# Batch-norm matmul on one core: the second block of w loaded ahead of the second half of the first chunk

## The chip, the cores and the metric

The kernel runs on one core of a Trainium2 chip. The metric is device time in microseconds of one execution, and the median over several executions is compared. The engines of the core are named as the profile names them: PE is TensorE (its matmuls; PEld are its weight loads), DVE is VectorE, ACT is ScalarE, POOL is GpSimd and SP is SyncE. POOL and SP issue the DMAs.

## What is computed

x holds 16 x 512 rows of 1024 numbers, weight is 1024 x 768, all float32. The product of all 8192 rows with the weight is normalised per output column over all rows:

```python
y = np.matmul(x, weight)
mean = np.mean(y, axis=(0, 1), keepdims=True)
var = np.var(y, axis=(0, 1), keepdims=True)
y_norm = (y - mean) / np.sqrt(var + eps)
return (gamma * y_norm + beta).astype(np.float32)
```

The statistics need every row, so nothing can be stored before the whole product is there. The kernel keeps the product on chip in bfloat16 and normalises it from there.

## The kernel before, in words

The 8192 rows are cut into 16 chunks of 512 rows (`CH`, `C`). The 768 output columns are six tiles of 128 (`NT`). The contraction over 1024 is cut into four blocks, counted by `jw`; a block has two halves (`e`), so that a full product of one output tile with one chunk is eight matmuls accumulating in one PSUM bank.

**Loads.** `load_x` (line 157) loads a range of rows with four DMAs from POOL, each of a quarter of the columns into 32 partitions, and the DMA converts to bfloat16. The first two chunks come in four loads of 256 rows each (called quarters of x below; the first two quarters are the two halves of chunk 0), the others in loads of 512 rows. `load_w` (line 145) loads one or more blocks of the weight, again with four DMAs from POOL. In all, w is loaded in three steps: block 0, block 1, and blocks 2 and 3 together. All these DMAs go out on one queue in program order; the framework gives them eight semaphores in turn, so a DMA is issued only when the one eight places before it has landed. That makes POOL wait, and what stands behind it on POOL waits too.

**Turning x.** x arrives with its rows on the partitions, while the matmuls need the contraction there; `turn_x` (line 164) transposes it on DVE, in squares of 32 x 32 pairs of bfloat16 numbers, into `xT`. For each half of chunk 0 there are two transposes: the first covers blocks 0 and 1, the second blocks 2 and 3.

**Matmuls.** `mm` (line 192) multiplies one output tile by one chunk, over a list of blocks and, for chunk 0, over a half of its rows: with `q0` and `q1` it covers 256 or all 512 columns of the moving operand. `mm_rows` (line 182) is the other form, with x as the stationary operand and 384 output columns at once; most chunks use it for the first three tiles. `wake` (line 151) runs matmuls on an idle tile that nobody reads, 30 at the very start and 8 (`FILL`) within chunk 0.

**The order.** Nothing is issued where it is written. Each piece of work is put into a list with a time that a small model in the code works out (`at`, line 441), the list is sorted by that time, and the pieces are then issued in that order; `seq` (line 77) ties each instruction behind the one before it on its engine. The model's times (2.7 us per 256 rows of x, 2.1 us per block of w and so on) decide only the order, never an actual wait. Lines 447 to 471 fix the order of the loads, and lines 497 to 510 that of chunk 0: `part(w, q0, q1, jws)` puts out the six tiles' matmuls for the halves q0 to q1 with the blocks `jws`, no earlier than the model has that block and those rows. Before the change the sequence on PE is: 30 idle matmuls, block 0 on the first half (12 matmuls of 256 columns), 8 idle matmuls, block 0 on the second half (12 of 256), block 1 on both halves at once (12 of 512), blocks 2 and 3 on both halves (24 of 512), then chunk 1.

**What follows.** Six tiles of chunk 0 fill six PSUM banks. As each is complete, DVE takes its statistics (`bn`) and ACT copies it out (`keep`). The remaining chunks follow on PE without a pause, the later tiles of chunks 5 to 15 last, while the finished tiles are normalised and stored.

Of the kernel before, what the change touches and what calls it, by code (L numbers as in the profile page):

```python
# [10 lines left out]
def kernel(  # L11
# [429 lines left out]
    def at(t, fn, *args):  # L441
        events.append((t, len(events), fn, args))
# [1 line left out]
    Q_US, MM_US, ROW_US = 2.7, 1.75, 1.31  # L444
    t = 1.0
    arrive = {}
    order = [("x", 0), ("w", 0, 1), ("x", 1), ("w", 1, 2), ("w", 2, 4)]
    order += [("x", q) for q in range(2, SHORT * QPC)] + [("c", c) for c in range(SHORT, C)]
    for kind, n, *n1 in order:
        if kind == "w":  # L450
# [46 lines left out]
    def part(w, q0, q1, jws):  # L497
        nonlocal pe
        pe = max(pe, arrive["w", w], arrive[q1 * QR // P - 1])
        for nt in range(NT):  # L500
            at(pe, mm, nt, 0, jws, q0, q1)
            pe += MM_US * len(jws) / JW * (q1 - q0) / QPC

    part(0, 0, 1, [0])
    at(pe, wake, FILL)
    part(0, 1, 2, [0])
    part(1, 0, 2, [1])
    pe = max(pe, arrive["w", 2])
    for nt in range(NT):
        unit(nt, 0, MM_US / 2, [2, 3])  # L510
# [148 lines left out]
```

## Time and profile before

| | |
|---|---|
| median of 6 runs | 217.39 us (217.07 to 217.72) |
| the profiled execution's own time | 217.72 us |
| its span, first to last instruction | 215.9 us |
| PE busy | 198.4 us, 92% of the span |
| DVE, ACT, POOL busy | 150.1, 124.0, 140.4 us |
| share of PE in the chain that ended last | 84% |
| start of the matmuls with blocks 2 and 3 | 20.07 us into the span |
| mean granted TensorE clock | 0.977 |

The profile shows one execution, times in microseconds from the first instruction. A row of the timeline merges instructions of one kind that follow one another: start, length, engine, line, operation with its tiles, the count, and in brackets how long the engine had been idle and what ended that. The chain of waits follows the last instruction back to what released it, step by step; it is read here in order of time. DMA rows name the tile written and the tensor read, with "landing" counted from the issue.

### The profile page before, as it was taken

What the parts mean: (1) busy time and instruction counts of PE and PEld (TensorE: products, weight loads), DVE (VectorE), ACT (ScalarE), POOL (GpSimd) and SP (SyncE); (2) the same over time, 40 slices, a digit from 0 to 9 for tenths busy, and PEclk for the clock granted to TensorE, in tenths of its full rate; (3) what the DMA queues carried; (4) which work ended last, traced back from release to release, by engine and by line L of the source; (5) the groups of instructions that cost most, each with busy time, mean ns of one, the idle gap of its engine ahead of it and who ended that gap; (6) DMA issues with size and microseconds to landing.
All of it is one profiled execution on the core that took longest, in us unless ns stands there. A gap on an engine that the chain in (4) does not pass through costs nothing.

```text
span 215.9 us, 3477 instructions
## 1 busy us (share of the span) xinstructions
PE 198.4 (92%) x1174; PEld 106.2 (49%) x1174; DVE 150.1 (70%) x261; ACT 124.0 (57%) x236; POOL 140.4 (65%) x158
## 2 busy tenths in 40 slices
PE   7797999999999999999999999999999999996900
PEld 2352454545455565566556554444445455554800
DVE  3220968886987999799854349988999896566800
ACT  2000563645464566357766513767759999987940
POOL 7786868678595999667558601999999996000000
PEclk9999999999999999999999999999999999999785
DMA  5999999999999999997000000689698999999997
GB/s 58 169 178 176 190 196 196 196 197 196 196 191 193 197 196 196 196 197 107 2 3 0 0 0 0 231 310 340 248 334 279 366 357 335 324 346 307 346 345 216
DMA packets 70178, 43.75 MB, mean 203 GB/s; under 512 B 4112, under 2 KB 69648, under 8 KB 70160
## 3 DMA queue, kind: packets, MB, share of 16 engines
q0 software_dynamic: 34624, 18.36, 62.3%
q1 hardware_dynamic: 35536, 25.18, 36.0%
q8 instruction: 9, 0.15, 0.3%
q14 instruction: 9, 0.07, 0.1%
HBM read 36.71 MB, written 25.17 MB: 287 GB/s over the span
## 4 chain that ended last, share of the span: by engine, by line
PE 84%; DMA 5%; POOL 3%; ACT 2%; issue 1%; DVE 0%; ACTq 0%; POOLq 0%
PE y_ps L196 44%; PE y_ps L186 31%; PE o_ps L414 7%; DMA w_sb<-in_weight_dram 3%; DMA ring<-in_x_dram 2%; POOL w_sb L149 2%; POOL ring L162 1%; ACT o_sb L427 1%; PE y_ps L332 1%; PE a_ps L274 1%; PE tot_ps L232 1%; ACT ring L427 0%; ACTq L654 0%; ACT y_sb L342 0%; DVE y_sb L400 0%
## 5 line engine op out<-in xcount | busy, mean ns | idle before, releaser
L196 PE MATMUL y_ps<-xT_sb,w_sb 128*128 128x512 bf16 (+1 forms) x460 | 111.4, 381 | 2.9 <-DMA w_sb<-in_weight_dram 2.6
L196 PEld LDWEIGHTS <-w_sb 128*128 128x128 bf16 x460 | 43.5, 96 | 59.0 <-issue 4.9
L186 PE MATMUL y_ps<-w_sb,xT_sb 128*128 128x384 bf16 x416 | 68.6, 326 | 0.0
L345 ACT CAST y_sb<-y_ps 128x512 bf16<-128x512 f32 x56 | 33.0, 589 | 47.0 <-DVE stats L318 44.8
L186 PEld LDWEIGHTS <-xT_sb 128*128 128x128 bf16 x416 | 40.7, 98 | 27.7
L162 POOL DMA_DIRECT2D ring<-in_x_dram x72 | 45.2, 634 | 12.6 <-DVE xT_sb L174 6.3
L318 DVE BATCH_NORM_STATS2 stats<-y_ps 128x6 f32<-128x512 f32 x55 | 37.2, 686 | 21.4 <-PE y_ps L196 21.4
L212 POOL TENSOR_TENSOR sum<-sum,sq_sb 128x384 f32<-128x384 f32 x41 | 41.1, 1002 | 15.2 <-ACT sq_sb L208 13.4
L174 DVE STREAM_TRANSPOSE xT_sb<-ring 128x1024 f32<-128x1024 f32 (+1 forms) x34 | 39.6, 1170 | 15.6 <-DMA ring<-in_x_dram 15.1
L291 POOL TENSOR_TENSOR ring<-ring,sum 128x768 f32<-128x768 f32 x19 | 34.6, 1847 | 12.0 <-DVE y_sb L390 12.0
L414 PE MATMUL o_ps<-ident,y_sb 128*128 128x128 bf16 x228 | 37.7, 230 | 2.1 <-DVE y_sb L400 2.1
L215 DVE TENSOR_TENSOR sum<-y_ps,sum 128x384 f32<-128x384 f32 x52 | 28.3, 544 | 12.6 <-ACT sq_sb L208 11.5
L208 ACT ACTIVATE sq_sb<-y_ps 128x384 f32<-128x384 f32 x52 | 25.5, 494 | 13.1 <-PE y_ps L186 10.0
L221 ACT CAST y_sb<-y_ps 128x384 bf16<-128x384 f32 x52 | 24.9, 478 | 12.3 <-DVE sum L215 12.3
L427 ACT CAST ring<-o_ps 128x1024 f32<-128x1024 bf16 (+1 forms) x22 | 21.1, 966 | 4.9 <-PE o_ps L414 3.6
L414 PEld LDWEIGHTS <-y_sb 128*128 128x128 bf16 x228 | 20.0, 103 | 4.1 <-DVE y_sb L400 2.2
L285 DVE TENSOR_TENSOR ring<-y_sb,a_ps 128x768 f32<-128x768 bf16 x19 | 17.7, 937 | 0.0
L379 ACT ACTIVATE y_sb<-y_sb,shift,scale 128x512 bf16<-128x512 bf16 x22 | 17.2, 815 | 0.0
L291 POOL TENSOR_TENSOR o_sb<-o_sb,sum 128x768 f32<-128x768 f32 x7 | 12.9, 1844 | 0.2 <-DVE o_sb L285 0.2
L155 PE MATMUL idle_ps<-idle_sb 128*128 128x512 bf16 x38 | 10.1, 430 | 1.2 <-DVE idle_sb L103 1.2
L390 DVE TENSOR_SCALAR y_sb<-y_sb,scale,shift 128x512 bf16<-128x512 bf16 x30 | 10.3, 405 | 0.0
L427 ACT CAST o_sb<-o_ps 128x512 f32<-128x512 bf16 (+1 forms) x17 | 8.1, 632 | 0.4 <-PE o_ps L414 0.2
(65 smaller groups left out, 53.4 us busy)
## 6 DMA issues: line engine op xcount, KB each, us to landing
ring<-in_x_dram POOLq DMA_DIRECT2D x56, 256.0 KB, 9.0
out_dram<-ring SPq DMA_DIRECT2D x25, 384.0 KB, 2.9
out_dram<-ring SPq DMA_DIRECT2D x16, 512.0 KB, 3.6
out_dram<-o_sb SPq DMA_DIRECT2D x15, 256.0 KB, 4.3
out_dram<-o_sb SPq DMA_DIRECT2D x7, 384.0 KB, 3.7
ring<-in_x_dram POOLq DMA_DIRECT2D x16, 128.0 KB, 5.5
w_sb<-in_weight_dram POOLq DMA_DIRECT2D x8, 96.0 KB, 5.0
w_sb<-in_weight_dram POOLq DMA_DIRECT2D x4, 192.0 KB, 6.1
```

The costliest lines, as they stand in the source:

```text
L162: seq(nc.gpsimd.dma_start(x_bf[32 * i:32 * i + 32], src[:, :, KQ * i:KQ * (i + 1)]))
L174: seq(nc.vector.transpose(dst[:, half, :, jw0:jw1], src[:, :, jw0:jw1]))
L186: seq(nc.tensor.matmul(y_ps, xT[c][:, jw, s * P:(s + 1) * P, e], w_sb[:, jw, e, 0:NA], start=(jw == 0 and e == 0), stop=(jw == JW - 1 and ...
L196: seq(nc.tensor.matmul(y_ps, w_sb[:, jw, e, nt * P:(nt + 1) * P], xT[c][:, jw, q0 * QR:q1 * QR, e], start=(jw == 0 and e == 0 and q0 == 0) ...
L208: seq(nc.scalar.activation(sq_sb, py["row", c, s][:, 0:NA], AF.Square))
L212: seq(eng.tensor_add(acc, acc, py.pop(("sq", c, s))))
L215: seq(nc.vector.tensor_add(sum1, py["row", c, s][:, 0:NA], sum1))
L291: seq(nc.gpsimd.tensor_add(o_sb, o_sb, sum1[:, None, :].to_broadcast([P, 2, NA])))
L318: seq(nc.vector.bn_stats(stats_of(nt)[:, i, :], py[nt, c]))
L345: seq(nc.scalar.copy(y(nt, c), py.pop((nt, c))))
L414: seq(nc.tensor.transpose(dst, src, ident))
L427: seq(nc.scalar.copy(o_sb, src))
```

## The change

In the order of the loads, block 1 of w changes places with the second quarter of x, which is the second half of chunk 0. On PE, block 1 is no longer multiplied with both halves of chunk 0 at once after everything else: it is multiplied with the first half right after block 0, ahead of the 8 idle matmuls, and with the second half right after block 0 on that half. In instructions, PE's 12 matmuls of 512 columns with block 1 become 24 of 256 columns, with 12 more weight loads, and the 8 idle matmuls come 12 matmuls later. On POOL, four DMA issues change places with four others. DVE, ACT and SP have the same instructions in the same order.

```diff
-    order = [("x", 0), ("w", 0, 1), ("x", 1), ("w", 1, 2), ("w", 2, 4)]
+    order = [("x", 0), ("w", 0, 1), ("w", 1, 2), ("x", 1), ("w", 2, 4)]
...
     part(0, 0, 1, [0])
+    part(1, 0, 1, [1])
     at(pe, wake, FILL)
     part(0, 1, 2, [0])
-    part(1, 0, 2, [1])
+    part(1, 1, 2, [1])
     pe = max(pe, arrive["w", 2])
```

## The prediction

> **What bounds the kernel now.** I read the chain of waits first, because it says which work a change at the start has to touch to be seen at the end. Its first lines in order of time, columns start, length, what:
>
> ```profile
> 2.58 5.29 DMA ring<-in_x_dram
> 7.87 0.28 issue
> 8.16 0.57 POOL ring L162
> ...
> 12.79 0.53 POOL w_sb L149
> 13.31 0.15 issue
> 13.46 6.47 DMA w_sb<-in_weight_dram
> 19.93 0.14 issue
> 20.07 5.58 PE y_ps L196 x24
> 25.65 5.20 PE y_ps L186 x32
> 30.85 5.42 PE y_ps L196 x24
> ```
>
> TensorE is the bound from 20.07 us on: from there until about 197 the chain is PE work and next to nothing else. Before that the bound is the loading. The last piece of the last load of w (blocks 2 and 3, called w2 here) is issued at 13.46 and lands at 19.93, and PE starts 0.14 later. So this change can move the time through one number: when PE may start the 24 matmuls with blocks 2 and 3. In the profile that is 20.07, set by the landing of w2. Everything behind it slides along.
>
> Next the timeline of the same stretch (start, length, engine, line, operation, count, and in brackets the idle time before it with what ended it):
>
> ```profile
> 5.68 1.17 POOL L162 DMA_DIRECT2D ring<-in_x_dram  x2
> 8.16 1.25 POOL L162 DMA_DIRECT2D ring<-in_x_dram  x2 [1.31 <-DMA ring<-in_x_dram]
> 9.40 3.92 POOL L149 DMA_DIRECT2D w_sb<-in_weight_dram  x7
> 10.60 1.52 PE L196 MATMUL y_ps<-xT_sb,w_sb 128*128 128x256 bf16 x12 [1.13 <-DMA w_sb<-in_weight_dram]
> 11.96 1.89 PE L155 MATMUL idle_ps<-idle_sb 128*128 128x512 bf16 x8
> 13.30 1.30 DVE L174 STREAM_TRANSPOSE xT_sb<-ring 128x512 f32<-128x512 f32 x2 [3.33 <-DMA ring<-in_x_dram]
> 14.07 4.54 PE L196 MATMUL y_ps<-xT_sb,w_sb 128*128 128x256 bf16 x24 [0.22 <-DVE xT_sb L174]
> 20.07 5.58 PE L196 MATMUL y_ps<-xT_sb,w_sb 128*128 128x512 bf16 x24 [1.46 <-DMA w_sb<-in_weight_dram]
> ```
>
> The reader is to see the last row: PE has done all that block 0 and block 1 allow by 18.61 and idles 1.46 us for w2. Whatever PE does earlier is worth nothing as long as it is done by 20.07. (The row at 14.07 is 12 matmuls of 256 columns and, from 15.70, 12 of 512.)
>
> **The loads.** All loads are issued on POOL, and the ninth DMA waits for the first to land, the tenth for the second, and so on: the 1.31 us in front of 8.16 is the third piece of the first half of x. Adding each issue's start to its own time to landing gives when the four pieces land: x's first half last at 8.5; w block 0 (w0) at 9.0, 9.5, 10.0, 10.5; x's second half (x1) at 11.2, 11.9, 12.5, 13.1; w block 1 (w1) at 13.7, 14.2, 14.7, 15.6; w2 at 17.1, 18.0, 19.0, 19.93. They land in the order of issue, 0.65 us apart for a piece of x (128 KB), 0.5 for a piece of w0 or w1 (96 KB) and 0.97 for one of w2 (192 KB), that is some 195 KB per us for all of them. Only two gaps are longer: 0.9 before the last piece of w1 and 1.5 before the first of w2, 0.4 + 0.5 = 0.9 us of stray time together. So from 8 us on a queue that is never empty lands its bytes one after the other, and w2 lands when all that is ahead of it has landed.
>
> **The change, part by part.**
>
> 1. On POOL the four issues of w1 go ahead of the four of x1. Nothing else on POOL, SP, DVE or ACT changes place. Issue times: the first two of w1 at 5.7 and 6.2; the third still waits for the first half of x and starts at 8.16, the fourth at 8.83; then x1, each waiting for a piece of w0 (the first until 9.0 + 0.28, the step from landing to issue that the chain shows at 7.87), 4 x 0.59 from 9.35 to about 11.75. w2 then waits for pieces of w1 that landed long ago (11.0 to 12.5) instead of for pieces of x1, and its four issues of 0.53 run 11.75 to 13.87: the first 0.28 later than before (11.47), the last 0.13 earlier (13.33 against 13.46). None of the four is near its landing (5.6 to 6.5 us after issue), so this should move w2's landing by nothing. If the 0.28 did open a hole in the queue it would cost 0.28; if the landing followed its issue it would gain 0.13. POOL's next issues, the third and fourth quarter of x, start at 14.0 as before (14.13); they now wait for x1, whose pieces land from 13.2 on, 0.3 us or more ahead of each; the later quarter waits for w2 as it did.
>
> 2. The landings. The bytes ahead of w2 are the same, so I take 19.93 again. w1 lands last at 10.5 + 4 x 0.5 = 12.5 (3.1 earlier), x1 last at 12.5 + 4 x 0.65 = 15.1, or 15.6 if the stray 0.5 falls to whoever stands there. Both ends for w2: without the stray time 15.1 + 4 x 0.97 = 19.0, 0.9 earlier; with as much again, 20.8, 0.9 later. The trace does not say what the stray time belongs to (a place in the queue, a change from pieces of x to pieces of w, chance), so I take the middle.
>
> The Trainium skill, "DMA: Bandwidth & Descriptors", section "Anatomy of one DMA — SWDGE (gpsimd) path", gives a DMA from this queue as about 2.0 us fixed plus its bytes over 436 GB/s. By it the last piece of w2 would land about 2.5 us after its issue (an estimate), near 15.8; PE's own work would then be the bound, and the sum would be the 0.2 us that part 4 finds for the narrower matmuls. The trace disagrees: 6.47 us, and 4.3 for the quickest of w1; the backlog sets it, so the sum goes by the rows.
>
> 3. PE, first half: 12 matmuls of 256 columns with w1 on the first half of chunk 0, at the start spacing of the 10.60 row (12 loads of weights in 1.26 us, so some 0.113 each): from 12.65 to 14.0. Then the 8 filling matmuls, 1.89 us as before, to 15.9.
>
> 4. PE, second half: needs x1 turned. Before, x1 landed at 13.13, DVE began at 13.30, the first transpose (0.69) covers blocks 0 and 1, and PE began at 14.07: 0.94 after landing. Now 16.05, or 16.5. DVE has nothing else to do until 21.17, so the later transpose delays nobody on DVE. Then 24 matmuls of 256 columns, 23 x 0.113 + 0.28 = 2.9 us: done at 18.9, or 19.4. Against the 12 of 512 columns that they replace in part (0.209 apart, 2.5 us), cutting block 1 in two adds 12 weight loads and about 0.2 us. All this ends 0.7 to 1.2 us ahead of 20.07, hidden under the wait for w2; without that cover the delay from 18.61 would show, at most 0.8.
>
> 5. The clock. Its granted value is 1.00 in every stretch from 0 to 28 us, across idle stretches of 1.13 and 1.46. The new idle stretches are 0.5 (before w1), about 0.2 (before x1) and 0.7 to 1.2 (before w2), none longer than what the trace shows to be harmless, so I charge nothing.
>
> **Sum.** 0 us: PE starts at 20.07 again and all behind it is the same. The profiled execution took 217.72 for a span of 215.9, 0.33 above the median of 217.39; a change of nothing against it is a median of 217.4.
>
> **The rivals.**
>
> A, faster: the stray time goes. For it: it lies in the passage from x1 by way of w1 to w2, which the change reorders. Against: x1 still hands over to pieces of w, now w2. If all 0.9 goes, w2 lands at 19.0, PE's own work (18.9 to 19.4) is then nearly the limit, and the time falls by 0.6 to 0.9: 216.5 to 216.8.
>
> B, slower: the second half of x becomes the last thing PE waits for. From the last landing of x1 at L, PE is done at L + 0.94 + 2.9 = L + 3.8; this decides once L is over 16.2 (20.07 less 3.8), against my 15.1 to 15.6. w2 stands behind x1 in the queue and needs another 3.9 itself, so a late x1 also makes w2 late. At L = 16.6 PE resumes at 20.5 to 20.7: 0.4 to 0.6 lost, 217.9 to 218.0; at 17.0 a whole microsecond. For it: the filling matmuls and the transposes now stand behind later data. Against: 0.6 us of room.
>
> C, slower: the order w0, w1, x1, w2 drains worse (a hole while POOL waits to 8.16 with pieces that are 96 instead of 128 KB, or more stray time). The pieces queued by 6.7 hold 64 KB less than before, 0.3 us of the queue; with part 1's 0.28 that is 0.6, and at the far end 0.9: 217.9 to 218.3.
>
> D, the change does not do what it says, since two of w1's four issues still wait to 8.16: w1 would land little earlier. It makes no odds to the time (PE waits for w2 anyway); counted with the first case.
>
> **How the numbers follow.** A measurement of this kernel tells 0.2%, 0.43 us, from no change. The first case, w2 within 0.43 us of its place, gets 0.44; A 0.24; B 0.16; C 0.16. So faster 0.24, same 0.44, slower 0.32. The likeliest is 217.4, alone 217.0 to 217.8. The range takes in most of A, and B and C up to 0.9 late: 216.6 to 218.3 leaves out about 0.06 at each end.
>
> **What would show it.** Right: the idle time of PE before the 512-column matmuls at about 20.1 still ended by the DMA of w, 0.7 to 1.2 us long; x1's first transpose at 15.3 to 15.8; PE's matmuls with block 1 from about 12.6. A wins if the 512-column matmuls start at 19.2 to 19.6, C if at 20.5 or later with a DMA of w as its releaser; B if PE's idle time there is gone. Wrong altogether if PE's work after 31 us no longer follows without idle time, or the granted clock in the first 28 us falls below 1.

## The result and the profile after

The changed kernel takes 218.69 us (median of 16 executions, 217.59 to 220.40) against 217.26 for the kernel before (37 executions): 0.71% slower, ratio 1.0071 with a 95% interval of 1.0054 to 1.0088. That is 1.4 us, where 0 was predicted and the range ended at 218.3.

The chain of waits of the changed kernel, in order of time (start, length, what):

```profile
3.15 5.67 DMA ring<-in_x_dram
8.82 0.28 issue
9.10 0.49 POOL w_sb L149
9.59 0.01 issue
9.60 1.72 POOL ring L162 x3
11.32 5.51 DMA ring<-in_x_dram
...
16.96 0.72 DVE xT_sb L174
17.68 0.04 issue
17.72 2.88 PE y_ps L196 x24
20.60 0.13 issue
20.73 5.58 PE y_ps L196 x24
26.31 5.20 PE y_ps L186 x32
```

The last load of w is gone from the chain. In its place stands the second half of x (x1): its last piece, issued at 11.32, lands at 16.83; DVE turns it, PE does its 24 narrow matmuls, and only then are blocks 2 and 3 taken up, at 20.73. The timeline shows the same on POOL, DVE and PE:

```profile
3.71 2.94 POOL L149 DMA_DIRECT2D w_sb<-in_weight_dram  x6
7.92 0.49 POOL L149 DMA_DIRECT2D w_sb<-in_weight_dram  x1 [1.26 <-DMA ring<-in_x_dram]
9.10 0.49 POOL L149 DMA_DIRECT2D w_sb<-in_weight_dram  x1 [0.69 <-DMA ring<-in_x_dram]
9.60 2.30 POOL L162 DMA_DIRECT2D ring<-in_x_dram  x4
12.78 1.52 PE L196 MATMUL y_ps<-xT_sb,w_sb 128*128 128x256 bf16 x12 [0.40 <-DMA w_sb<-in_weight_dram]
14.14 1.89 PE L155 MATMUL idle_ps<-idle_sb 128*128 128x512 bf16 x8
16.96 1.31 DVE L174 STREAM_TRANSPOSE xT_sb<-ring 128x512 f32<-128x512 f32 x2 [6.71 <-DMA ring<-in_x_dram]
17.72 8.59 PE L196 MATMUL y_ps<-xT_sb,w_sb 128*128 128x256 bf16 x48 [1.69 <-DVE xT_sb L174]
```

Block 1 did come early: PE works with it from 12.78. But x1 is issued from 9.60 on instead of 5.68, and is turned at 16.96 instead of 13.30. In this profile w2 (blocks 2 and 3) also landed at 20.60, so both paths end together: w2 stands behind x1 in the queue and came 3.8 us after it.

One rule of thumb makes the profiles comparable. The span is the start of the matmuls with blocks 2 and 3 plus 195.8 to 195.9 us: 20.07 and 215.9 before, 20.73 and 216.6 after. The time of an execution is its span plus 1.8. By this rule the median of before stands for a start at 19.6, and that of the changed kernel at 21.0. The rule holds as long as TensorE's clock is not lowered. Both profiled executions are off their medians, that of before 0.5 us above (217.72) and that of the changed kernel 0.3 below (218.38).

### The profile page after: what moved, and what is told of

It is laid out like the page before. It is cut to its first block, busy times and chain, and to the rows that moved or that the text cites. A ratio compares the mean times of both kernels' runs of the same rounds, so it can differ in the third digit from the quotient of the medians.

```text
span 216.6 us, 3501 instructions
## 1 busy us (share of the span) xinstructions
PE 198.5 (92%) x1186; PEld 106.1 (49%) x1186; DVE 150.1 (69%) x261; ACT 123.6 (57%) x236; POOL 140.4 (65%) x158
## 4 chain that ended last, share of the span: by engine, by line
PE 83%; DMA 5%; ACT 3%; POOL 2%; issue 1%; ACTq 0%; DVE 0%; DVEq 0%; POOLq 0%
PE y_ps L196 46%; PE y_ps L186 31%; DMA ring<-in_x_dram 5%; PE o_ps L414 4%; ACT o_sb L427 2%; POOL ring L162 2%; PE y_ps L332 1%; ACT ring L427 1%; PE a_ps L274 1%; PE tot_ps L232 1%; ACTq L655 0%; DVE xT_sb L174 0%; POOL w_sb L149 0%; ACT y_sb L342 0%; ACT std L367 0%
## 5 line engine op out<-in xcount | busy, mean ns | idle before, releaser
L196 PEld LDWEIGHTS <-w_sb 128*128 128x128 bf16 x472 | 44.7, 96 | 58.3 <-issue 5.1
L162 POOL DMA_DIRECT2D ring<-in_x_dram x72 | 45.2, 634 | 12.5 <-DVE xT_sb L174 6.1
L174 DVE STREAM_TRANSPOSE xT_sb<-ring 128x1024 f32<-128x1024 f32 (+1 forms) x34 | 39.6, 1170 | 19.8 <-DMA ring<-in_x_dram 19.4
L414 PEld LDWEIGHTS <-y_sb 128*128 128x128 bf16 x228 | 18.7, 97 | 5.4 <-DVE y_sb L400 2.2
L390 DVE TENSOR_SCALAR y_sb<-y_sb,scale,shift 128x512 bf16<-128x512 bf16 x30 | 10.3, 402 | 0.0
```

What stands on the lines that cost most here:

```text
L162: seq(nc.gpsimd.dma_start(x_bf[32 * i:32 * i + 32], src[:, :, KQ * i:KQ * (i + 1)]))
L174: seq(nc.vector.transpose(dst[:, half, :, jw0:jw1], src[:, :, jw0:jw1]))
L196: seq(nc.tensor.matmul(y_ps, w_sb[:, jw, e, nt * P:(nt + 1) * P], xT[c][:, jw, q0 * QR:q1 * QR, e], start=(jw == 0 and e == 0 and q0 == 0) ...
L414: seq(nc.tensor.transpose(dst, src, ident))
```

## The experiments

The question was what makes x1 late. The first theory, the hole: POOL may have eight DMAs under way, and with pieces of w (96 KB) in place of pieces of x (128 KB) ahead, x1 is issued late and the queue runs short, so that it drains slowly. (A piece is one of the four DMAs of a load.) The rival, the stretch: from 11 to 16 us the small packets of x are slow whatever stands in the queue. A third, the clock: PE's longer idle time halves its clock in some executions.

**Loads alone.** Only the issues of block 1 move; PE's order and the model's times stay.

```diff
-            at(t, load_w, n, *n1)
+            at(5.75 if n == 1 else t, load_w, n, *n1)
```

> Only the loads change places; PE keeps the order of before (block 0 on both halves, then block 1 on both at once). If the late landing of the second half of x is the whole cause, PE has 12 matmuls of 512 columns and 12 of 256 left when x is turned at 17.7 us into the span instead of 24 of 256: 1.4 + 2.6 = 4.0 instead of 2.9, so PE takes up blocks 2 and 3 some 1.0 later than in the changed kernel (about 21.7), and the time is 0.8 to 1.2 us above the changed kernel's, 219.4 to 219.9. If PE's new order (24 narrow matmuls, the filling ones later) is the cause, this kernel is back at the time of before within 0.4 us.

221.19 us, ratio 1.0197 (1.0159 to 1.0235), worse than either expectation. The last piece of x1 landed at 17.25, so the loads alone reproduce the delay. The rest, in this profile (222.35 us, the slowest of the six executions), is the clock. The columns are the stretch, its length, the busy time (and count of instructions) of PE, PEld, DVE, ACT and POOL, the granted clock, the busy share of the DMA engines, and GB/s:

```profile
13.00:16.60 3.60, 0.48 (x3) 0.10 (x1) 0.00 (x0) 0.00 (x0) 1.88 (x5) 1.00 1.14 143
16.60:20.00 3.40, 1.86 (x9) 1.27 (x9) 1.30 (x2) 0.00 (x0) 2.30 (x4) 0.50 1.14 202
20.00:23.40 3.40, 3.40 (x12) 1.46 (x10) 0.00 (x0) 0.00 (x0) 2.57 (x5) 0.50 1.44 193
```

PE idles 4.66 us for x1, until 18.14, and the clock is halved from 16.6 to 23.4. So PE does its first 5.3 us of work at half speed, which costs 2.6 us. PE's new order in the changed kernel softens this: it has 24 narrow matmuls left at that point instead of 12 narrow and 12 wide, and its idle time is shorter.

**PE's order alone.** The load order put back in the changed kernel.

```diff
-    order = [("x", 0), ("w", 0, 1), ("w", 1, 2), ("x", 1), ("w", 2, 4)]
+    order = [("x", 0), ("w", 0, 1), ("x", 1), ("w", 1, 2), ("w", 2, 4)]
```

> Only PE's order changes (block 1 on the first half ahead of the filling matmuls, then both blocks on the second half); the loads keep the order of before. Then PE waits for block 1, which lands at 14.4 to 15.6 in the two profiles of before, with work on the second half of x standing ready behind it: 12 matmuls (1.4), filling (1.9), 24 matmuls (2.9), so blocks 2 and 3 are taken up at 20.7 to 21.9 instead of 18.5 to 20.1, and the time is about 2 us above before, 218.8 to 219.6; more where the wait of about 2.5 us halves the clock. If PE's order were free, the time would be that of before.

220.21 us, ratio 1.0144 (1.0092 to 1.0197), of four executions: above the 218.8 to 219.6 expected, which allowed for more if the clock was halved. PE waits as expected, and it is halved, here from 16.4 to 19.9:

```profile
15.39 1.82 PE L196 MATMUL y_ps<-xT_sb,w_sb 128*128 128x256 bf16 x12 [3.32 <-DMA w_sb<-in_weight_dram]
17.01 3.30 PE L155 MATMUL idle_ps<-idle_sb 128*128 128x512 bf16 x8
```

The 8 filling matmuls take 3.30 instead of 1.89 us, and the 24 narrow ones begin at 20.15. Each half of the change alone costs more than both together. The load order here is that of before, and yet w2 landed at 20.12, with 1.4 and 1.6 us before its first two pieces where 0.9 to 1.0 is usual.

**More filling.** `FILL = 16` in the changed kernel.

> The changed kernel with 16 filling matmuls instead of 8: they run 1.9 us longer, from 14.1 to about 17.9, and cover the idle time of PE (15.99 to 17.72 in the profile of the changed kernel) in which PE waits for the second half of x. Clock theory (in some executions the idle time halves the clock for a window): the executions near 219.7 with a mean clock of 0.964 to 0.966 disappear, the median falls by 0.3 us or more, below 218.4. Landing theory alone: the filling ends 0.2 us after x is turned, and the time is 0.0 to 0.3 us above the changed kernel's, with the same share of low clocks.

218.39 us, ratio 1.0061 (1.0039 to 1.0083). Against the first median of the changed kernel, 218.69, that is just the fall of 0.3 that the clock theory asked for. But the next experiment, on the same chip, gives 218.56 for the changed kernel itself, 0.17 apart. No low clock showed in 12 executions, but none showed in the 9 of the changed kernel there either. So the run does not settle the clock's share. It does show that filling the idle time leaves most of the loss, 1.35 us against before.

**The changed kernel again.** No edit.

> The changed kernel once more, for a second profile. If the late landing of the second half of x belongs to the order of the loads, its last piece lands between 16.3 and 17.3 again and its rate between 12 and 15 us is 120 to 160 GB/s again; if it was chance in one execution, it lands near 15.1 to 15.6. The time is 218.2 to 219.2 in either case.

218.56 us, ratio 1.0080 (1.0055 to 1.0105). x1 landed at 16.83 once more and PE took up blocks 2 and 3 at 20.72. The delay is no chance of one profile: in all five profiles with this load order (these two, loads alone, more filling, no filling) the four pieces of x1 took 4.0 to 5.3 us.

**Blocks 0 and 1 in one load.** The second block is still ahead of x1, but in pieces twice as large, so that x1 is issued as early as in the kernel before.

```diff
-    WAKE = 30
+    WAKE = 42
...
-    order = [("x", 0), ("w", 0, 1), ("x", 1), ("w", 1, 2), ("w", 2, 4)]
+    order = [("x", 0), ("w", 0, 2), ("x", 1), ("w", 2, 4)]
...
-    part(0, 0, 1, [0])
+    part(0, 0, 1, [0, 1])
     at(pe, wake, FILL)
-    part(0, 1, 2, [0])
-    part(1, 0, 2, [1])
+    part(0, 1, 2, [0, 1])
```

> Blocks 0 and 1 of w in one load of four DMAs of 192 KB, then the second half of x, then blocks 2 and 3; PE starts with both blocks on the first half (42 idle matmuls ahead instead of 30, to cover the longer wait). The eight DMAs that may be under way now hold 1280 KB instead of 896 KB plus waiting, so the second half of x is issued from about 6 us on, as in the kernel before, and not from 9.6. Hole theory (the queue runs empty because the window of eight holds the smaller pieces of w and the second half of x is issued late): x lands by 15.3, blocks 2 and 3 by 20.0, and the time is that of before within 0.4 us or less. Stretch theory (from 11 to 16 us the pieces of x are slow whatever stands in the queue): x lands at 16.3 or later and the time is 0.5 to 1.5 us above before.

217.44 us, ratio 1.0026 (1.0004 to 1.0048). x1 was issued from 5.81 and landed at 15.02, blocks 2 and 3 at 18.78. That rules out the stretch: pieces of x moved at full rate between 11 and 15 us. It fits the hole, though size of the pieces and time of issue were changed together. The stretches side by side, first the changed kernel (same columns as above, the last is GB/s):

```profile
8.00:10.50 2.50, 1.69 (x8) 0.58 (x6) 1.30 (x2) 0.00 (x0) 1.80 (x4) 1.00 1.06 200
10.50:13.00 2.50, 1.74 (x14) 1.31 (x15) 0.00 (x0) 0.00 (x0) 2.50 (x6) 1.00 1.08 140
13.00:15.50 2.50, 2.50 (x19) 1.60 (x17) 0.00 (x0) 0.00 (x0) 2.31 (x6) 1.00 1.14 141
```

and the kernel with both blocks in one load:

```profile
8.00:10.50 2.50, 2.50 (x14) 1.09 (x12) 1.30 (x2) 0.00 (x0) 1.58 (x3) 1.00 1.09 207
10.50:13.00 2.50, 2.20 (x13) 1.08 (x12) 0.00 (x0) 0.00 (x0) 1.45 (x3) 1.00 1.30 191
13.00:15.50 2.50, 2.50 (x23) 2.02 (x22) 0.36 (x1) 0.00 (x0) 2.41 (x7) 1.00 1.24 208
```

Both load x1 right behind blocks 0 and 1, and in both the last piece of block 1 lands at 12.3 to 12.7. The one moves 140 GB/s from 10.5 to 15.5, the other 191 and 208. The changed kernel's DMA engines are not empty in that time, though: their busy share is 1.08 and 1.14, against 1.30 and 1.24, and no half microsecond between 8 and 17 us moves less than 87 GB/s. This kernel is still 0.3% above before for a reason of its own: its 8 filling matmuls run to 17.06, while x1 is turned at 15.9.

**The same with 3 filling matmuls.** `FILL = 3`.

> The kernel with blocks 0 and 1 in one load of 192 KB pieces, with 3 filling matmuls instead of 8. In its profile with 8 the filling ran until 17.06, while the second half of x was turned at 15.9 and blocks 2 and 3 had landed at 18.78: PE took them up at 19.8 after its own 24 matmuls. With 3 filling matmuls PE begins the 24 at 15.95 and is done at 18.9, just after blocks 2 and 3 land. If the landing is now as steady as in that profile, the time is 0.6 to 0.9 us below that kernel (217.44), 216.5 to 216.9, and at or below before. If it is not, and blocks 2 and 3 land nearer to 20, the time stays at 217.2 to 217.5.

216.84 us against 217.05 for before, ratio 0.9998 (0.9981 to 1.0016). The fall of 0.6 us is the one expected (blocks 2 and 3 landed at 18.68), and it brings the kernel level with before, not ahead.

**The kernel before again.** No edit.

> The kernel before once more, for a second profile. The time of every profile so far is the start of the matmuls with blocks 2 and 3 plus 195.9 us of span. By that rule the median of before (217.0 to 217.3) stands for a start at 19.4 to 19.6, so this profile should show blocks 2 and 3 landing earlier than 19.93, at 19.0 to 19.6, with less than the 0.9 us of stray time. If they land at 19.9 again, the rule is wrong and something else makes up the difference between the profiles (0.7 us) and the medians (1.4 us).

217.05 us, ratio 1.0000 (0.9980 to 1.0021). The profiled execution took 216.12, and its chain of waits reads

```profile
12.74 5.60 DMA w_sb<-in_weight_dram
18.34 0.14 issue
18.47 5.58 PE y_ps L196 x24
```

with a span of 214.3: 18.47 plus 195.9. The rule holds. The landing, 18.34, is earlier than the 19.0 to 19.6 expected, as the execution was itself 0.9 faster than the median. So blocks 2 and 3 landed at 18.3 in one execution and at 19.9 in another of the same kernel, and the profile that the prediction was made from was a late one. That profile was 0.5 us above its median and the changed kernel's 0.3 below: this is why the two lie 0.7 us apart and the medians 1.4.

**Half of block 1 ahead.** Two of its four pieces are issued before x1, two after.

```diff
-    def load_w(jw, jw1):
+    def load_w(jw, jw1, i0=0, i1=4):
...
-        for i in range(4):
+        for i in range(i0, i1):
...
-            at(t, load_w, n, *n1)
+            if n == 1:
+                at(5.75, load_w, n, *n1, 0, 2)
+                at(t, load_w, n, *n1, 2, 4)
+            else:
+                at(t, load_w, n, *n1)
```

> The kernel before, with only two of the four pieces of block 1 issued ahead of the second half of x, the other two after it; PE's order as before. The pieces of x are then issued at about 7.9, 8.8, 9.4 and 10.0 instead of 5.7, 6.3, 8.2, 8.8 (before) or 9.6 to 11.3 (changed kernel). Hole theory (the later they are issued, the shorter the queue and the slower they land): x lands at 14.3 to 16.0, between before (13.1) and the changed kernel (16.4 to 17.3); the time is 0.2 to 1.2 us above before. If the order (x behind any w) is what slows x down, it lands at 15.7 or later as in the changed kernel. If neither, it lands at 14.1 and the time is that of before.

218.18 us, ratio 1.0063 (1.0034 to 1.0092). The pieces of x1 were issued at 7.95, 9.18, 9.76 and 10.3 and landed at 12.44, 13.12, 15.20 and 15.84: the first two 0.7 us apart, then a gap of 2.1. The last lies between before and the changed kernel, as the hole has it, but 15.84 also meets the other case (15.7 or later). Against "x behind any w" speak the first two pieces, which followed w at full rate. And since the gap stands before one piece alone, not every piece issued late is slow.

**x1 late, nothing of block 1 ahead.** POOL adds zeros to its zeroed sum three times before the issues of x1; the order of the loads is that of before.

```diff
+    def delay(count):
+        for _ in range(count):
+            seq(nc.gpsimd.tensor_add(sum2, sum2, sum2))
...
+    at(5.75, delay, 3)
     at(1.0, wake, WAKE)
```

> The kernel before with its order of loads, but POOL adds zeros to its zeroed sum three times (about 3 us) ahead of the four issues of the second half of x, so that they go out at about 9.4 to 11.1 as in the changed kernel, with nothing of block 1 ahead of them. Only the landing of the four pieces counts here, the time must be worse (all later loads are late too, 219.5 to 222). Hole theory: late issue alone slows them, and the four land 0.8 us or more apart, the last at 15.8 to 17.3. Order theory: with no w ahead they land 0.65 apart, the last 4.0 us after its issue, at about 15.0.

219.48 us in two executions. x1 went out from 8.54 on (the additions took 0.83 each) and landed at 11.68, 12.59, 13.56 and 14.87, 0.9 to 1.3 us apart and 4.6 us after the last issue. Since it went out earlier than planned, the last landing is below the 15.8 expected by the hole theory, and near the 15.0 of its rival. The spacing is what the hole theory said, with nothing of block 1 ahead of x1:

```profile
8.00:10.50 2.50, 2.09 (x11) 0.88 (x10) 1.30 (x2) 0.00 (x0) 2.50 (x5) 1.00 0.58 96
10.50:13.00 2.50, 2.50 (x19) 1.59 (x18) 0.00 (x0) 0.00 (x0) 2.50 (x6) 1.00 1.17 149
13.00:15.50 2.50, 0.35 (x2) 0.17 (x2) 0.51 (x1) 0.00 (x0) 1.78 (x4) 1.00 1.10 155
```

The queue runs dry here (49 and 18 GB/s in the two halves of the microsecond from 9 to 10), and what is issued then does not come at 190 but at 150. The changed kernel shows no such empty stretch, so this run shows that late issue into an empty queue is slow, and not that the changed kernel's queue was empty.

**No filling.** The changed kernel with `FILL = 0`.

> The changed kernel with none of the 8 filling matmuls: PE then idles from about 14.1 to 17.7 us, 3.6 instead of 1.7. Clock theory (an idle time of PE of this length halves the granted clock for a while, and the executions of the changed kernel at 219.5 and above with a mean clock near 0.965 are those in which 1.7 was already enough): nearly all executions now show a mean clock of 0.965 or less, the profile shows a granted clock of 0.5 for some microseconds before 25, and the time is 0.7 to 2 us above the changed kernel's. If the clock does not matter, the time is that of the changed kernel, 218.3 to 218.8, since the filling ends before x is turned.

219.71 us, ratio 1.0093 (1.0064 to 1.0122); by the ratios that is 0.3 to 0.5 us above the changed kernel (1.0080 and 1.0071), at the edge of what these intervals tell apart. The ratio leaves out the two longest executions; by the medians of all the distance is 0.7 to 0.8, the lower end of the 0.7 to 2 that the clock theory asked for. The mean clock of the ten executions ran from 0.958 (220.86 us) to 0.977 (217.57), and it was 0.965 or less in five, not in nearly all. The mean is a poor sign, though: the profile, one of the better executions (218.47 us, mean 0.970), has the halved clock too:

```profile
13.00:16.10 3.10, 0.53 (x5) 0.30 (x4) 0.12 (x1) 0.00 (x0) 2.40 (x6) 1.00 1.20 177
16.10:19.51 3.41, 2.76 (x14) 1.87 (x14) 1.19 (x2) 0.00 (x0) 2.26 (x4) 0.50 1.12 201
19.51:22.00 2.49, 2.42 (x17) 1.62 (x17) 0.15 (x1) 0.00 (x0) 1.99 (x5) 1.00 1.44 193
```

An idle time of 3.2 us halves the clock for 3.4. So the clock can be lost here, and in the executions with the lowest clock the time is 220.5 to 221.4. It is not what the changed kernel loses in all its executions: its two profiles have the full clock and still take up blocks 2 and 3 at 20.7.

**Chunk 0 in one load, and then with blocks 2 and 3 apart.** Two tries for a kernel ahead of both, from the one with blocks 0 and 1 together. Chunk 0 comes in four pieces of 256 KB and PE begins with all of it; in the second try, blocks 2 and 3 come as two loads, and PE does block 2 first.

```diff
-    order = [("x", 0), ("w", 0, 2), ("x", 1), ("w", 2, 4)]
+    order = [("c", 0), ("w", 0, 2), ("w", 2, 4)]
...
-                at(tx, turn_x, m0, 0, 0, JW // 2)
-                at(tx + 0.1, turn_x, m0, 0, JW // 2, JW)
+                at(tx, turn_x, m0, i * QR // 32, 0, JW // 2)
+                at(tx + 0.1, turn_x, m0, i * QR // 32, JW // 2, JW)
...
-    part(0, 0, 1, [0, 1])
-    at(pe, wake, FILL)
-    part(0, 1, 2, [0, 1])
+    part(0, 0, 2, [0, 1])
```

and for the second try, on top:

```diff
-    order = [("c", 0), ("w", 0, 2), ("w", 2, 4)]
+    order = [("c", 0), ("w", 0, 2), ("w", 2, 3), ("w", 3, 4)]
...
-            pe += MM_US * len(jws) / JW * (q1 - q0) / QPC
+            pe += 0.7
...
-    pe = max(pe, arrive["w", 2])
-    for nt in range(NT):
-        unit(nt, 0, MM_US / 2, [2, 3])
+    for jw in (2, 3):
+        pe = max(pe, arrive["w", jw])
+        for nt in range(NT):
+            unit(nt, 0, 0.43, [jw])
```

> Chunk 0 in one load of four DMAs of 256 KB, then blocks 0 and 1 in 192 KB pieces, then blocks 2 and 3; PE begins with blocks 0 and 1 on all of chunk 0 (24 matmuls of 512 columns). If the number of bytes that eight DMAs hold decides how fast the start drains, this holds the most (1792 KB): no stretch after 8 us under 180 GB/s, blocks 2 and 3 land at 18.0 to 18.7, and the time is 216.0 to 216.8, below before. If not, it is at before (217.0) or above.

> As the kernel with chunk 0 whole, but blocks 2 and 3 come as two loads of 96 KB pieces, and PE does all of block 2 before block 3, so that PE has work from about 12.5 us on without a wait for the last landing. If the pieces land as steadily (block 2 by 16.5, block 3 by 18.6), PE is done with chunk 0 about 23.3 us into the span instead of 24.9 (19.4 + 5.6, before) and the time is 1.0 to 1.7 us below before, 215.4 to 216.2. If the smaller pieces again leave too few bytes under way, a stretch of 120 to 160 GB/s comes back between 11 and 17 us, PE waits for block 3, and the time is 216.3 to 217.3.

220.35 us, ratio 1.0126 (1.0092 to 1.0160), and 219.83, ratio 1.0100 (1.0068 to 1.0131). Both expected times failed. In the first, loads ran at 180 to 227 GB/s from 9 us until 22 and blocks 2 and 3 landed at 18.60, as expected; but blocks 0 and 1 now stand behind all of chunk 0 and landed at 14.86, PE idled 2.31 us after its 42 idle matmuls, and the clock was halved from 16.0 to 19.4. In the second, the slow stretch came back behind the smaller pieces, 103 to 138 GB/s between 17.5 and 19 us; the clock fell there too (0.5 from 14.2 to 17.6). The times of the model in the code also moved a few instructions on DVE and POOL in these two.

## Why the prediction was wrong

The table gathers the landings, in us into the span: when the first piece of x1 is issued, when the load ahead of it has landed, when x1 has, how long its four pieces took, and when blocks 2 and 3 had landed.

| kernel | x1 issued from | load ahead landed | x1 landed | four pieces | w2 landed |
|---|---|---|---|---|---|
| before, first profile | 5.68 | 10.47 | 13.18 | 2.7 | 19.93 |
| before, again | 5.69 | 9.74 | 12.46 | 2.7 | 18.34 |
| both blocks in one load | 5.81 | 12.32 | 15.02 | 2.7 | 18.78 |
| changed | 9.60 | 12.65 | 16.83 | 4.2 | 20.60 |
| changed, again | 9.52 | 12.58 | 16.83 | 4.3 | 20.58 |
| changed, no filling | 8.81 | 11.87 | 15.86 | 4.0 | 19.60 |

- **What bounds the kernel**: right. In every profile with the clock at 1.00 the span followed the start of the matmuls with blocks 2 and 3, and PE's work behind it did not change.
- **Part 1, POOL's issues**: nearly right, 7.92 and 9.10 for the last two pieces of block 1 and 9.60 for x1, against 8.16, 8.83 and 9.35. What was drawn from it was wrong: "should move w2's landing by nothing", or 0.28 if a hole opened. It looked at w2's issues and not at x1's.
- **Part 2, the landings**: the step that failed. Block 1 landed at 12.65 (12.5 predicted). x1 was to need 4 x 0.65 = 2.6 and land at 15.1, or 15.6; it needed 4.2 and landed at 16.83. w2 then needed 3.8, where 3.9 was predicted, so its landing at 20.60 is x1's delay carried on: of the sum without stray time (19.0) the term for x1 alone was 1.6 too small. The premise was a queue that lands its bytes one after the other, at 195 KB per us for all. The runs show that this rate is not a constant of the queue: x1 issued from 9.6 drains at 140. The profile of before had a warning: the first half of x, issued into an empty queue, landed at 4.7, 5.9, 7.9 and 8.5, 1.3 us apart.
- **Part 2, the baseline**: 19.93 was taken for w2's place, with 0.9 us of stray time in it. Another execution of the same kernel has 18.34 and almost none, with block 0 landed 0.7 us earlier as well. The 0.9 was no property of the kernel to be carried over. It hid part of the loss: the changed kernel's 20.73 is 0.7 later than that profile's 20.07, but 1.1 later than the 19.6 that the median of before stands for.
- **Parts 3 and 4, PE**: the durations held (0.94 predicted and 0.89 measured from the landing to PE's start, 2.9 and 2.88 for the 24 matmuls; before the change the landing was at 13.18, not 13.13, so that the step was 0.89 there too). The cover was to be 0.7 to 1.2 us; none was left, since PE ended at 20.60.
- **Part 5, the clock**: 1.00 in the profile, as said, with an idle time of 1.69 that part 5 had put at 0.2. Of the 17 executions of the changed kernel five have a mean clock of 0.964 to 0.966 and take 219.5 to 220.4; the median of the other twelve is 218.5. That would put some 0.2 of the 1.4 us down to the clock. No profile caught such an execution, and the runs with more and with no filling could not settle it, so this share is argued, not shown. The two profiles with the full clock account for 1.1 of the 1.4 us.
- **The rivals**: B named the place (x1 last, deciding once it lands after 16.2, and the price of a microsecond at 17.0), and its sign came: PE's idle time before blocks 2 and 3 is gone. C named worse draining of this order ("a hole while POOL waits to 8.16"); its price of 0.6 to 0.9 us was too low, and the hole itself is not what the profile shows. Told apart as two cases they got 0.32 together; here one brought the other. A did not come: with the order of before, one profile has the stray time and another almost none.

What stays open is why x1 drains slowly when it is issued late. The bytes ahead of it do not explain it: when its first piece was issued, 672 KB of w were still to land in the changed kernel, and 640 KB of x and w in the second profile of before, where x1 came at the full rate. One rival was not tested: DVE turns the first half of chunk 0 (8.94 to 10.25 in the changed kernel) while POOL issues x1. In all the profiles with a slow x1 two of its issues fall into that time, in those with a fast one only one. Against it, pieces of x1 issued after DVE was done, at 10.76 and 11.32 in the changed kernel, still landed 1.0 us apart. No run here tells these apart.

## What to carry to other kernels

When loads are moved past each other on a queue that allows a fixed number of DMAs under way, look at the time of issue and not only at the order: small pieces ahead delay the issue of the large ones behind. Do not take the rate of the steady part for a load that will be issued later than before: here the same four pieces took 2.7 us or 4.2. At the 1.3 us per piece of the same profile's start, that term would have been 5.1 and the far end of the forecast about 218.9 (an estimate), which holds the result. And before a wait is taken as the place that will hold, look for its spread: one profile of a start that is bound by loads can be a microsecond off the median.

## What the hardware showed that was not expected

- Four pieces of x, 512 KB in all, landed in 2.7 to 2.8 us when they were issued from 5.7 us on (five profiles), and in 4.0 to 5.3 us when issued from 8.8 us or later behind eight pieces of w (five profiles). In the stretches of 2.5 us that were read, that is 175 to 208 GB/s against 122 to 141.
- The same kernel lands its first 2.6 MB of loads at 18.3 us in one profile and at 19.9 in another, and this accounts for the whole distance of the two executions (216.12 and 217.72).
- In the first 25 us, an idle time of PE of 2.3, 2.4, 2.6, 3.2, 3.3 and 4.7 us came with a granted clock halved for 3.4 us or twice that, each in one profile. 1.7 us did not in two, nor did 2.75 us in the profile of the kernel with half of block 1 ahead (mean clock 0.984), so its length alone does not decide.
